# A two-stream encoder layer on one core: the gate input and the gate's mix rows kept in SBUF, the pivot subtracted behind the update, the first norm's mean taken off first

## The chip, the core and the metric

The kernel runs on one core of a Trainium2 chip. The metric is device time of one execution in microseconds. Three executions of the kernel before took 1427.2 (the median), 1424.3 and 1427.87 us. One more was taken with the hardware profiler.

## The reference: what is computed

One layer of a streaming encoder, for a prompt of 1024 frames and for 32 frames of a running stream, with the same weights, all in float32, model width 1024. The input is modulated, projected, handed to three groups of heads (an mLSTM with a matrix memory, FoX attention with forget gates, and a gated MLP), joined, projected back, and normalised; a SwiGLU block with a second norm follows.

```python
h = x * (1 + sc1) + sh1
mq, mk, mv, mo, mi, mf, fq, fk, fv, ff, gu, gv = jnp.split(h @ w_in, split_at, axis=-1)
...
vn = _layer_norm(gv, gmlp_ln_g, gmlp_ln_b)
hg = _spatial_gate(gu, vn, gmlp_ws, gmlp_bs)   # 128 frames at a time, 4 groups of 64 channels
mix = jnp.concatenate([hm.reshape(B, S, D_MLSTM).astype(dt),
                       hf.reshape(B, S, D_FOX).astype(dt), hg], axis=-1) @ w_o
x = _layer_norm(ALPHA * x + (1 + g1) * mix, ln1_g, ln1_b)
h = x * (1 + sc2) + sh2
y = (jax.nn.silu(h @ w_gate) * (h @ w_up)) @ w_down
x = _layer_norm(ALPHA * x + (1 + g2) * y, ln2_g, ln2_b)
```

The states of the heads and vn of the 32 running frames are outputs too.

## The kernel before, in words

**Operands.** Every large product is made of three: operand and weight are split into a high part (a cast, L106 for weights) and a low part (a subtract, L107), and PE adds high*high, high*low and low*high (L118 to L120 in gemm, L283 to L285 in tm_unit) into one PSUM bank. Banks are few: three of pool pg ("g"), two of pt ("t"), two for the heads' scores and one for their output.

**Frames.** The 1056 frames (1024 of the prompt and 32 running) are nine tiles of 128 for the projections into rows (tm units), and two groups of columns for all that follows: group 0 is the prompt's first half, 512 frames in two cuts of 256; group 1 is the rest, 544 frames in two cuts of 272.

**Stages.** First the modulation and the input projection. Then a list sets the order in which units are emitted: fm units give fox's q and k (q0 to q7), tm units give values and gates, f0 to f7 are fox heads and m0 to m3 mLSTM tiles, both for group 0, whose working tiles lie in a pool mx0:

```python
ORDER = "q0 f0 q1 a f1 a q2 f2 k0 k1p s a q3 f3 a v q4 f4 a q5 f5 o a m0 q6 f6 a m1 q7 m2 f7 a m3"
```

When the list is done, mx0 is closed, and the pools ph (operands of the output projection), pz (residual z) and p2 (small tiles "tmp", "sil" and others) are opened on the memory that is free then. Now z is loaded (wo_res), the operand tiles hh and hl are made, and mix rows k = 0 to 5 are loaded from the DRAM tensor dmix and split into hh and hl (wo_mix, L888 the cast and L889 the subtract). Four tm units follow: gv for tiles 0 to 3 (evac_gv), gmlp for tiles 0 to 3 (evac_gmlp), then both for tiles 4 to 8; two fm units for group 1; then mix rows 6 and 7 by wo_mix; then the output projection wo of group 0, one tile of 128 rows (m) and one cut after another, its first norm ln1, the mixers of group 1 with the first products of the SwiGLU block between (up), its second product (down), and in the middle of that block group 1's wo and ln1.

**Who sets the order.** The program is written in that order, but a scheduler at build time fixes the order of each engine by when it expects operands. So a unit emitted later can run between the rows of an earlier one, which mostly holds here: while fox and mLSTM wait for DVE and ACT, PE runs the tm units. An engine then runs its rows strictly in that order. A tile in a pool that takes over freed memory waits for the last reader of the tiles that it covers (reuse by tile).

**The gate.** evac_gv normalises one tile of gv: statistics and the product on DVE (L353, into a "traw" tile, of which there are two), gain (L354) and offset (L355) on POOL, then a store to the DRAM tensor dvn. evac_gmlp loads that tile again ("gvn"), copies u out of its bank (L645, "traw"), mixes 128 frames with four matmuls per tile (L650) and multiplies (L653). to_mix transposes the result (L632), copies it to "mixs" (L634) and stores it to dmix.

**The sublayer's end and the norms.** sublayer_end takes a wo or down bank: DVE's L927 adds bank times gate into z. To keep the sums of squares small, z carries a pivot: row tile m = 0 gives a mean over its 128 rows (L837 on PE, L838 on ACT), which is subtracted from z's tile 0 by DVE (L839) and from every other tile by POOL (L924), there ahead of L927. ln_sum gathers sums (L849) and squares (L851). ln_stats makes from them r, the reciprocal deviation (L863 to L869), and e = -mean * r (L870); ln1 then runs per k: z times r (L942, DVE), plus e (L943, six on DVE and two on POOL), scale and shift (L946, ACT), high part (L950, ACT), low part (L951, DVE), which are operands of up (up_g). ln1_res (L960) prepares z for the next residual.

## Time and profile before

| what | us |
|---|---|
| three executions, median | 1427.2 |
| the profiled execution's own time | 1432.34 |
| its span in the trace | 1430.6 |
| PE busy | 1366.2 |
| DVE busy | 1046.7 |
| ACT busy | 657.2 |
| POOL busy | 269.3 |
| f6's transposes to m3's in the trace | 310.7 to 364.6 |
| first matmul of group 0's wo | 389.1 |
| first wait of PE behind group 0's ln1 | 472.4 |
| group 0's last down group, PE's wait | 889 to 890.75 |

The span is that of one profiled execution on the core; the profiled execution's own time has 1.7 us more around it. Busy time is the time in which an engine has at least one instruction running; matmuls overlap in the pipeline, so a full PE has no gap between them. The rows of the trace name an engine, a line of the kernel, the tile written and the tiles read, without their serial numbers.

### The profile page before, as it was taken

How to read it: one execution, taken by the hardware profiler on the slowest of the kernel's cores; microseconds unless marked ns; L12 is line 12 of the kernel's file. 1: busy time of each engine (PE TensorE's matmuls, PEld its weight loads, DVE VectorE, ACT ScalarE, POOL GpSimd, SP SyncE). 2: the span in 40 equal slices, each digit the busy share in tenths (PEclk: the TensorE clock that was granted, in tenths of full speed). 3: DMA queues.
4: the chain of work that ended last, by engine and by line, in shares of the span. 5: the costliest groups of instructions: out<-in, count | busy, mean ns of one | idle time of the engine just before them, and what ended most of it. 6: DMA issues, size and time to landing. Idle time of an engine off the chain costs nothing.

```text
span 1430.6 us, 28812 instructions
## 1 busy us (share of the span) xinstructions
PE 1366.2 (96%) x10937; PEld 1312.7 (92%) x10937; DVE 1046.7 (73%) x2359; ACT 657.2 (46%) x1392; POOL 269.3 (19%) x313
## 2 busy tenths in 40 slices
PE   7999999999999899999999999999999999999994
PEld 4799988989889789999999998999898999999994
DVE  5548655678678677687777764678878877878777
ACT  3323234434445564546555453335655444536353
POOL 0103200043167300000000001174611000000343
PEclk9999999999999999999999998999999999999997
DMA  9754678465754745344343423565666666534231
GB/s 360 248 207 133 193 210 257 159 213 168 226 172 157 210 161 178 110 150 122 119 146 103 101 86 73 194 176 151 184 160 187 178 175 185 149 125 133 75 118 63
DMA packets 135986, 233.02 MB, mean 163 GB/s; under 512 B 22548, under 2 KB 79516, under 8 KB 135848
## 3 DMA queue, kind: packets, MB, share of 16 engines
q1 hardware_dynamic: 130952, 221.74, 48.9%
q0 software_dynamic: 4896, 9.44, 4.5%
q8 instruction: 86, 1.41, 0.4%
q14 instruction: 52, 0.43, 0.1%
HBM read 197.24 MB, written 52.76 MB: 175 GB/s over the span
## 4 chain that ended last, share of the span: by engine, by line
PE 75%; DVE 10%; DMA 8%; ACT 3%; issue 2%; SPq 1%; POOL 0%; DVEq 0%; ACTq 0%
PE up_g L119 5%; PE up_g L120 5%; PE up_g L118 5%; PE dn_g L118 4%; PE dn_g L119 3%; PE dn_g L120 3%; PE tm_g L283 3%; PE tm_g L284 3%; PE tm_g L285 3%; PE fm_g L118 3%; PE fm_g L119 2%; PE fm_g L120 2%; PE fox_t L733 2%; PE wo_g L120 2%; PE wo_g L118 2%
## 5 line engine op out<-in xcount | busy, mean ns | idle before, releaser
L119 PE MATMUL up_g<-wo_al,up_whi 128*128 128x256 f32 (+1 forms) x736 | 211.7, 288 | 3.8 <-DVE wo_al L951 3.8
L118 PE MATMUL up_g<-wo_ah,up_whi 128*128 128x256 f32 (+1 forms) x736 | 210.3, 287 | 3.9 <-ACT lna_tmp L946 3.3
L120 PE MATMUL up_g<-wo_ah,up_wlo 128*128 128x256 f32 (+1 forms) x736 | 210.4, 286 | 0.9 <-DVE up_wlo L107 0.9
L118 PEld LDWEIGHTS up_g<-wo_ah,up_whi 128*128 128x128 f32 x736 | 139.6, 190 | 5.4 <-ACT wo_ah L950 3.5
L119 PEld LDWEIGHTS up_g<-wo_al,up_whi 128*128 128x128 f32 x736 | 139.8, 190 | 5.0 <-DVE wo_al L951 4.2
L120 PEld LDWEIGHTS up_g<-wo_ah,up_wlo 128*128 128x128 f32 x736 | 139.7, 190 | 1.6 <-DVE up_wlo L107 1.4
L284 PE MATMUL tm_g<-tm_wlo,start_h1h 128*128 128x256 f32 (+1 forms) x384 | 110.6, 289 | 0.0
L285 PE MATMUL tm_g<-tm_whi,start_h1l 128*128 128x256 f32 (+1 forms) x384 | 110.3, 288 | 0.0
L283 PE MATMUL tm_g<-tm_whi,start_h1h 128*128 128x256 f32 (+1 forms) x384 | 109.8, 287 | 0.2 <-ACT tm_mixs L634 0.2
L118 PE MATMUL fm_g<-start_h1h,fm_whi 128*128 128x256 f32 (+2 forms) x344 | 102.2, 302 | 6.9 <-DVE fm_qkl L368 2.0
L118 PE MATMUL dn_g<-up_acth,dn_whi 128*128 128x256 f32 (+1 forms) x352 | 103.5, 295 | 2.7 <-DVE mlstm_z L927 2.4
L119 PE MATMUL dn_g<-up_actl,dn_whi 128*128 128x256 f32 (+1 forms) x352 | 101.6, 289 | 0.0
L120 PE MATMUL dn_g<-up_acth,dn_wlo 128*128 128x256 f32 (+1 forms) x352 | 101.6, 289 | 0.0
L119 PE MATMUL fm_g<-start_h1l,fm_whi 128*128 128x256 f32 (+2 forms) x344 | 101.6, 295 | 0.0
L120 PE MATMUL fm_g<-start_h1h,fm_wlo 128*128 128x256 f32 (+2 forms) x344 | 100.9, 295 | 0.0
L1057 ACT CAST sup_whi<-sup_raw 128x1024 fp32r<-128x1024 f32 x51 | 52.8, 1048 | 84.3 <-DVE sup_raw L1064 27.8
L107 DVE TENSOR_TENSOR up_wlo<-up_raw,up_whi 128x1024 fp32r<-128x1024 f32 x56 | 71.4, 1276 | 24.7 <-ACT up_whi L106 24.4
L106 ACT CAST up_whi<-up_raw 128x1024 fp32r<-128x1024 f32 x56 | 58.7, 1048 | 56.7 <-PE dn_g L119 20.6
L736 ACT CAST fox_pth<-fox_t 128x256 fp32r<-128x256 f32 (+3 forms) x144 | 51.0, 373 | 68.3 <-PE fox_t L733 63.4
L1058 DVE TENSOR_TENSOR sup_wlo<-sup_raw,sup_whi 128x1024 fp32r<-128x1024 f32 x51 | 63.9, 1256 | 18.5 <-ACT sup_whi L1057 18.4
L118 PEld LDWEIGHTS fm_g<-start_h1h,fm_whi 128*128 128x128 f32 x344 | 65.4, 192 | 12.4 <-ACT start_h1h L223 3.1
L737 DVE TENSOR_TENSOR fox_ptl<-fox_t,fox_pth 128x256 fp32r<-128x256 f32 (+3 forms) x144 | 58.0, 417 | 23.7 <-ACT fox_pth L736 22.5
(560 smaller groups left out, 4662.9 us busy)
## 6 DMA issues: line engine op xcount, KB each, us to landing
up_raw<-w_gu SPq DMA_DIRECT2D x56, 512.0 KB
dn_raw<-w_dn SPq DMA_DIRECT2D x28, 512.0 KB
ada_late<-w_ada SPq DMA_DIRECT2D x24, 512.0 KB
wo_raw<-w_o SPq DMA_DIRECT2D x24, 512.0 KB
start_dp<-w_gu SPq DMA_DIRECT2D x18, 512.0 KB
start_dp<-w_gu POOLq DMA_DIRECT2D x18, 512.0 KB, 7.1
sup_raw<-w_gu SPq DMA_DIRECT2D x17, 512.0 KB
sup_raw<-start_dp SPq DMA_DIRECT2D x17, 512.0 KB
```

The lines of the kernel that those rows point to most:

```text
L106: nc.scalar.copy(hi[:, :w], raw[:, :w])
L107: (eng or nc.vector).tensor_tensor(lo[:, :w], raw[:, :w], f(hi[:, :w]), ALU.subtract)
L118: nc.tensor.matmul(ps, hi, xh(k), start=start and k == 0, stop=False)
L119: nc.tensor.matmul(ps, hi, xl(k), start=False, stop=False)
L120: nc.tensor.matmul(ps, lo, xh(k), start=False, stop=stop and k == n - 1)
L283: nc.tensor.matmul(ps[:, :ncol], xh, hi, start=k == 0, stop=False)
L284: nc.tensor.matmul(ps[:, :ncol], xh, lo, start=False, stop=False)
L285: nc.tensor.matmul(ps[:, :ncol], xl, hi, start=False, stop=k == 7)
L736: nc.scalar.copy(ph[:, lo:nq], ps[:, lo:nq])
L737: nc.vector.tensor_tensor(pl[:, lo:nq], ps[:, lo:nq], f(ph[:, lo:nq]), ALU.subtract)
L1057: nc.scalar.copy(h, x)
L1058: tt(l, x, f(h), ALU.subtract)
```

## The change

The line numbers of the changed kernel are shifted: L355 becomes L360, L632 L636, L650 L660, L839 L849, L924 L961, L927 L958, L942 L975, L951 L983.

1. The offset of the gate norm is added into a tile that stays: for tiles 0 to 7 halves of "sil" tiles of p2 (two buffers, a tag that other units use later), for tile 8 a "gvn" tile. The nine stores to dvn and nine loads are gone; evac_gmlp reads the tile.
2. For tiles 0 to 3 of the gate to_mix writes the transposed rows straight into hh (ACT) and hl (DVE) at k = 6 and 7. Their four stores to dmix, four loads, and wo_mix(0, (6, 7)) with four casts and four subtracts are gone.
3. The pivot is subtracted on POOL behind L927 instead of ahead of it, in wo and in down's last group, for both groups of frames.
4. ln1 uses a new ln_center: ACT copies the mean to SBUF, and while r is being made, the mean is taken off z's eight tiles, on DVE and POOL in turn; behind r a single product per k is left. L870 and L943 are gone.

```diff
--- before.py
+++ after.py
@@ -352,10 +352,14 @@
         v = self.t(self.sm, [P, 256], F32, "traw", 2)
         nc.vector.tensor_scalar(v[:n], ps[:n, :256], mv[:n, 0:1], r[:n], ALU.subtract, ALU.mult)
         nc.gpsimd.tensor_tensor(v[:n], v[:n], self.rowp[:n, 272:528], ALU.mult)
-        nc.gpsimd.tensor_tensor(v[:n], v[:n], self.rowp[:n, 528:784], ALU.add)
-        self.store(self.dvn[:n, tt, :], v[:n])
         if tt == 8:
-            self.store(self.d["o_vn"], v[:n])
+            self.vn[tt] = self.t(self.sm, [P, 256], F32, "gvn", 1)
+        elif tt % 2 == 0:
+            x = self.t(self.p2, [P, 544], F32, "sil", 2)
+            self.vn[tt], self.vn[tt + 1] = x[:, :256], x[:, 256:512]
+        nc.gpsimd.tensor_tensor(self.vn[tt][:n], v[:n], self.rowp[:n, 528:784], ALU.add)
+        if tt == 8:
+            self.store(self.d["o_vn"], self.vn[tt][:n])
 
     def evac_qk(self, h):
         nc = self.nc
@@ -630,6 +634,13 @@
         ps = bank or self.t(self.pt, [P, 512], F32, "t")
         for i in range(2):
             nc.tensor.transpose(ps[:, i * P:i * P + L], x[:L, i * P:(i + 1) * P], self.ident[:L, :L])
+        if k0 == 6 and j < 4:
+            a = j // 2 * 256
+            y = ps[:, :256].rearrange("p (i q) -> p i q", i=2)
+            hi, lo = (z[0][a][:, 6:8, j * P - a:(j + 1) * P - a] for z in (self.hh, self.hl))
+            nc.scalar.copy(hi, y)
+            nc.vector.tensor_tensor(lo, y, f(hi), ALU.subtract)
+            return
         s = self.t(pool, [P, 2, P], F32, "mixs", 2)
         nc.scalar.copy(s[:, :, :L], ps[:, :256].rearrange("p (i q) -> p i q", i=2)[:, :, :L])
         c = min(j // 4, 1)
@@ -639,8 +650,7 @@
 
     def evac_gmlp(self, tt, ps, n, bank=None):
         nc = self.nc
-        vn = self.t(self.sm, [P, 256], F32, "gvn", 2)
-        self.load(vn[:n], self.dvn[:n, tt, :])
+        vn = self.vn[tt]
         u = self.t(self.sm, [P, 256], F32, "traw", 2)
         nc.scalar.copy(u[:n], ps[:n, :256])
         bank = bank or ps
@@ -850,6 +860,29 @@
                               z[:, m, sl], ALU.add)
         nc.vector.tensor_tensor(st["qs"][:, sl], st["qs"][:, sl], sq, ALU.add)
 
+    def ln_center(self, st, z, sl, sub):
+
+        nc = self.nc
+        n = sl.stop - sl.start
+        pm = self.t(self.pt, [P, 512], F32, "t")[:, :n]
+        nc.tensor.matmul(pm, self.onesm, st["zs"][:, sl], start=True, stop=True)
+        pq = self.t(self.pt, [P, 512], F32, "t")[:, :n]
+        nc.tensor.matmul(pq, self.onesm, st["qs"][:, sl], start=True, stop=True)
+        mean = st["zs"][:, sl]
+        nc.scalar.copy(mean, pm)
+        v = self.t(self.p2, [P, 272], F32, "tmp", 4)[:, :sl.stop - sl.start]
+        nc.scalar.activation(v, pm, AF.Square)
+        nc.vector.scalar_tensor_tensor(v, pq, self.epsa, v, ALU.add, ALU.subtract)
+        r = st["pv"][:, sl]
+        nc.scalar.activation(r, v, AF.Ln)
+        nc.scalar.activation(r, r, AF.Exp, scale=-0.5)
+        nc.vector.scalar_tensor_tensor(v, v, -0.5, r, ALU.mult, ALU.mult)
+        nc.vector.tensor_tensor(v, v, r, ALU.mult)
+        nc.vector.scalar_tensor_tensor(r, v, 1.5, r, ALU.add, ALU.mult)
+        for k in range(KT):
+            (nc.gpsimd if sub[k] == "p" else nc.vector).tensor_tensor(z[:, k, sl], z[:, k, sl], mean, ALU.subtract)
+        return r
+
     def ln_stats(self, st, sl):
 
         nc = self.nc
@@ -920,12 +953,12 @@
 
         sl = slice(a, b)
         pivot = st and st["pivot"]
-        if pivot and m:
-            self.nc.gpsimd.tensor_tensor(z[:, m, sl], z[:, m, sl], st["pv"][:, sl], ALU.subtract)
         g = self.modcol(gate, m)
         for x, y, i in self.parts(c, a, b):
             self.lastz = self.nc.vector.scalar_tensor_tensor(z[:, m, x:y], ps[:, x - a:y - a], g[i], z[:, m, x:y],
                                                              ALU.mult, ALU.add)
+        if pivot and m:
+            self.nc.gpsimd.tensor_tensor(z[:, m, sl], z[:, m, sl], st["pv"][:, sl], ALU.subtract)
         if pivot and m == 0:
             self.ln_pivot(st, z, sl)
         if st and st["sum"]:
@@ -934,13 +967,12 @@
     def ln1(self, c, st, a, b):
         self.phase = f"lna{c}"
         nc, z, hh, hl, sl = self.nc, self.z[c], self.hh[c][a], self.hl[c][a], slice(a, b)
-        r, e = self.ln_stats(st, sl)
+        r = self.ln_center(st, z, sl, "vpvpvpvp")
         for k in range(KT):
             yield
             self.phase = f"lna{c}"
             zk = z[:, k, sl]
             nc.vector.tensor_tensor(zk, zk, r, ALU.mult)
-            (nc.gpsimd if k % 4 == 1 else nc.vector).tensor_tensor(zk, zk, e, ALU.add)
             h = self.t(self.p2, [P, 272], F32, "tmp", 4)[:, :b - a]
             for x, y, i in self.parts(c, a, b):
                 nc.scalar.activation(h[:, x - a:y - a], z[:, k, x:y], AF.Identity, bias=self.lnb[:, k, i:i + 1],
@@ -1163,7 +1195,7 @@
         self.dmqk = t([P, 4, T], "dmqk")
         self.dmv = t([P, 9, 256], "dmv")
         self.dmo = t([P, 9, 256], "dmo")
-        self.dvn = t([P, 9, 256], "dvn")
+        self.vn = {}
         self.dfs = t([8, 6, S], "dfs")
         self.dsf = t([8, 2, PAST + NS], "dsf")
         self.dM = t([4, 9, P], "dM")
@@ -1277,7 +1309,6 @@
         for h in range(QD, PRE):
             self.fm_unit(w3[2 + h], self.evac_qk(h), (1,))
         s6.close()
-        self.wo_mix(0, self.KORDER[6:])
         self.pn = self.pool("pn")
         self.ln_consts()
         st = self.ln_begin(nc.gpsimd)
```

**PE, between fox's f6 and mLSTM's m3.** Rows of PE's order in the kernel before, behind the transposes of f6 and the first mLSTM products; fox_, mlstm_ and ada_ tiles belong to the list's units, tm_g is a bank of a tm unit, tm_gvn the reloaded gate input:

```order
L650 MATMUL tm_g_4638<-tm_gvn_4663,start_wsp_176 128x64 x4
L284 MATMUL tm_g_4680<-tm_wlo_4593,start_h1h_168 128x256
L285 MATMUL tm_g_4680<-tm_whi_4592,start_h1l_169 128x256
L283 MATMUL tm_g_4680<-tm_whi_4592,start_h1h_168 128x256
L284 MATMUL tm_g_4680<-tm_wlo_4593,start_h1h_168 128x256
L285 MATMUL tm_g_4680<-tm_whi_4592,start_h1l_169 128x256
L632 MATMUL tm_g_4596<-start_ident_120,tm_traw_4623 128x128 x2
L584 MATMUL mlstm_s_3942<-mlstm_mv_740_3905,mlstm_mkw_3929 128x130 x2
L186 MATMUL ada_t_3878<-start_ident_120,ada_adas_3891 128x128 x2
L553 MATMUL mlstm_s_4076<-mlstm_mqb_4055,mlstm_mqk_4053 128x256 x2
L632 MATMUL tm_g_4638<-start_ident_120,tm_traw_4665 128x128 x2
L283 MATMUL tm_g_4722<-tm_whi_4586,start_h1h_168 128x256
```

And in the changed kernel the end of that stretch, from f7's last products (fox_o) over m3's last rows (mlstm_t_4329) to the first tm row:

```order
L565 MATMUL mlstm_t_4282<-start_ident_119,mlstm_mqk_4255 128x128 x2
L748 MATMUL fox_o_4190<-fox_ptl_4223,fox_v_4136 64x128
L753 MATMUL fox_o_4190<-fox_pth_4222,fox_v_4136 128x128
L757 MATMUL fox_o_4190<-fox_pth_4196,fox_v_4136 128x512
L186 MATMUL ada_t_4234<-start_ident_119,ada_adas_4247 128x128 x2
L588 MATMUL mlstm_s_4298<-mlstm_mv_835_4261,mlstm_mkw_4285 128x130 x2
L636 MATMUL mlstm_t_4329<-start_ident_119,mlstm_mhm_4309 128x128 x2
L283 MATMUL tm_g_4632<-tm_whi_4583,start_h1h_167 128x256
L284 MATMUL tm_g_4632<-tm_wlo_4584,start_h1h_167 128x256
```

From f6's transposes to the L636 row there is no tm row left in the changed order: the tm banks from tm_g_4632 on, 296 matmuls of 128x256 with nine tiles of L660 and L636, stand behind it.

**POOL, over the same stretch.** In the kernel before, L354 (gain) and L355 (offset) of a gate tile stand together; mlstm_ rows are the list's units:

```order
L354 TENSOR_TENSOR tm_traw_4456<-tm_traw_4456,start_rowp_175 128x256
L355 TENSOR_TENSOR tm_traw_4456<-tm_traw_4456,start_rowp_175 128x256
L354 TENSOR_TENSOR tm_traw_4497<-tm_traw_4497,start_rowp_175 128x256
L355 TENSOR_TENSOR tm_traw_4497<-tm_traw_4497,start_rowp_175 128x256
L107 TENSOR_TENSOR tm_wlo_4593<-tm_raw_4590,tm_whi_4592 128x1024
```

In the changed kernel L360 is the offset, written to a "sil" tile (the gains L354 of the first two tiles, tm_traw_4455 and tm_traw_4496, stand further ahead):

```order
L546 TENSOR_TENSOR mlstm_mo_4061<-mlstm_mo_4061,start_rowp_174 128x256
L535 MEMSET mlstm_mv_835_4261 128x4
L546 TENSOR_TENSOR mlstm_mo_4264<-mlstm_mo_4264,start_rowp_174 128x256
L360 TENSOR_TENSOR tm_sil_4458<-tm_traw_4455,start_rowp_174 128x256
L360 TENSOR_TENSOR tm_sil_4458<-tm_traw_4496,start_rowp_174 128x256
L354 TENSOR_TENSOR tm_traw_4536<-tm_traw_4536,start_rowp_174 128x256
L354 TENSOR_TENSOR tm_traw_4577<-tm_traw_4577,start_rowp_174 128x256
```

The first two offsets moved behind the gates (mlstm_mo) of m2 and m3, and the third and fourth gate tile's rows behind them.

**DVE, at group 0's last down group.** In the kernel before, up_pv is the pivot and dn_g a bank of down:

```order
L107 TENSOR_TENSOR dn_wlo_12360<-dn_raw_12357,dn_whi_12359 128x1024
L839 TENSOR_TENSOR mlstm_z_856_4347<-mlstm_z_856_4347,up_pv_12152 128x256 x2
L927 SCALAR_TENSOR_TENSOR mlstm_z_856_4347<-dn_g_12195,start_mod_155,mlstm_z_856_4347 128x256
L927 SCALAR_TENSOR_TENSOR mlstm_z_856_4347<-dn_g_12231,start_mod_155,mlstm_z_856_4347 128x256
L927 SCALAR_TENSOR_TENSOR mlstm_z_856_4347<-dn_g_12261,start_mod_155,mlstm_z_856_4347 128x256
```

In the changed kernel:

```order
L107 TENSOR_TENSOR dn_wlo_12317<-dn_raw_12314,dn_whi_12316 128x1024
L958 SCALAR_TENSOR_TENSOR mlstm_z_855_4346<-dn_g_12188,start_mod_154,mlstm_z_855_4346 128x256
L958 SCALAR_TENSOR_TENSOR mlstm_z_855_4346<-dn_g_12203,start_mod_154,mlstm_z_855_4346 128x256
L849 TENSOR_TENSOR mlstm_z_855_4346<-mlstm_z_855_4346,up_pv_12109 128x256
L958 SCALAR_TENSOR_TENSOR mlstm_z_855_4346<-dn_g_12218,start_mod_154,mlstm_z_855_4346 128x256
L958 SCALAR_TENSOR_TENSOR mlstm_z_855_4346<-dn_g_12233,start_mod_154,mlstm_z_855_4346 128x256
```

Two updates moved ahead of the first cut's subtract L849, and the second cut's subtract moved further back.

## The prediction

> **What bounds the kernel now.** I read the page first, then the table of stretches around the stages that the change touches, then the waits of the tensor engine, and last single pieces of the timeline. The page:
>
> ```profile
> span 1430.6 us, 28812 instructions
> PE 1366.2 (96%) x10937; PEld 1312.7 (92%) x10937; DVE 1046.7 (73%) x2359; ACT 657.2 (46%) x1392; POOL 269.3 (19%) x313
> PE   7999999999999899999999999999999999999994
> PEclk9999999999999999999999998999999999999997
> ```
>
> PE is busy 96% of the span, in nearly every slice. So the kernel is bound by PE's own stream, and a change can pay only through the 64 us in which PE stands idle, or through the clock. It can cost without such a limit, wherever it leaves PE without work. PE's waits on what the change touches:
>
> ```profile
> engine line waited for: us in total, times, longest us
> PE up_g L119 <- DVE wo_al L951: 3.8, 2, 3.2
> PE up_g L118 <- ACT lna_tmp L946: 3.3, 1, 3.3
> PE dn_g L118 <- DVE mlstm_z L927: 2.4, 2, 1.8
> PE tm_g L650 <- DMA tm_gvn<-start_dvn: 1.9, 1, 1.9
> PE wo_g L118 <- DVE mlstm_z L927: 1.3, 1, 1.3
> PE wo_g L118 <- ACT wo_whi L106: 1.0, 1, 1.0
> PE wo_g L120 <- DVE wo_wlo L107: 0.8, 1, 0.8
> ```
>
> **Part 1, the gate input in SBUF: a loss.** This is the term that decides. By the order of instructions, the gate unit's matmuls (tm_g: input projection L283 to L285, token mix L650, transposes L632) are spread in before between the last fox and mLSTM units (f6, m1, m2, f7, m3). In the changed kernel all of them but the first three gate tiles stand behind m3's last transposes. The reason lies in the code: the add of the gate norm now writes a "sil" tile of pool p2, which is opened on the memory of the fox/mLSTM pool mx0 after that is closed. The first such add (POOL) must wait until the tiles under it are read for the last time. Behind it on POOL stand the next tiles' L354 and adds; the two "traw" buffers stay full, so DVE's L353 of the next tiles waits, their PSUM banks stay taken, and PE has no bank to fill.
>
> What that stretch holds in before, from f6's transposes (310.7 us) to m3's (364.6). The first row is of the stretches (its length, then busy time of PE, PEld, DVE, ACT and POOL with their counts, granted clock, DMA share, GB/s), the next five are PE's groups on tm_g (count, then least, median and greatest ns, first and last start), the last two of the timeline:
>
> ```profile
> 310.70:364.60 53.90, 53.76 (x448) 50.12 (x447) 45.97 (x159) 23.61 (x64) 16.45 (x19) 1.00 0.50 152
> L285 PE MATMUL tm_g<-tm_whi,start_h1l x79: 276/282/367, 310.5 to 362.9; 128*128 128x256 f32 x79
> L283 PE MATMUL tm_g<-tm_whi,start_h1h x78: 274/282/367, 310.6 to 359.1; 128*128 128x256 f32 x78
> L284 PE MATMUL tm_g<-tm_wlo,start_h1h x78: 276/282/369, 310.8 to 359.2; 128*128 128x256 f32 x78
> L650 PE MATMUL tm_g<-tm_gvn,start_wsp x48: 217/275/323, 317.4 to 363.8; 128*128 128x64 f32 x48
> L289 PE MATMUL tm_g<-tm_whi,start_hs x8: 276/278/467, 345.2 to 347.2; 128*64 128x256 f32 x8
> 366.18 0.28 PE L283 MATMUL tm_g<-tm_whi,start_h1h 128*128 128x256 f32 x1
> 366.30 0.28 PE L284 MATMUL tm_g<-tm_wlo,start_h1h 128*128 128x256 f32 x1
> ```
>
> PE is full there (53.76 of 53.90 us). Matmuls of this shape start 0.12 us apart. The filler is 78 + 78 + 79 + 16 (the rows of the short tile, L288 to L291, together) = 251 x 0.119 = 29.9 us; the 48 of L650 and eight transposes (L632) at about 0.11 = 6.0. Together 35.9. What remains, 53.8 - 35.9 = **17.9 us, is the fox and mLSTM units' own PE work**.
>
> How long does the stretch take without filler? It is a chain through DVE, ACT and PE, and DVE carries most. DVE's rows there:
>
> ```profile
> L653 DVE SCALAR_TENSOR_TENSOR tm_traw<-tm_g,start_colp,tm_traw 128x64 f32<-128x64 f32 x23 | 5.1, 277 | 1.4 <-PE tm_g L650 1.3
> L737 DVE TENSOR_TENSOR fox_ptl<-fox_t,fox_pth 128x512 fp32r<-128x512 f32 (+3 forms) x8 | 3.8, 480 | 1.3 <-ACT fox_pth L736 1.3
> L548 DVE SCALAR_TENSOR_TENSOR mlstm_mw<-mlstm_mb,start_col,start_maskbig 128x128 f32<-128x128 f32 x8 | 3.1, 444 | 1.9 <-PE mlstm_s L569 1.9
> L591 DVE SCALAR_TENSOR_TENSOR fm_C<-fm_C,fm_d0c,mlstm_s 64x65 f32<-64x65 f32 x8 | 2.2, 280 | 0.1
> L188 DVE TENSOR_REDUCE ada_adam<-ada_t 128x4 f32<-128x16 f32 x1 | 0.2, 173 | 0.0
> L539 ACT ACTIVATE mlstm_mo<-mlstm_mo 128x256 f32<-128x256 f32 x2 | 0.8, 417 | 2.5 <-DMA mlstm_mo<-start_dmo 2.5
> ```
>
> The groups of tm_ and fm_wlo tiles (first row: L653) sum to 19.2 us. The other 28 groups (second row to the L188 row) sum to 34.6, and a third L591 block of 1.1 that now also comes ahead of the filler makes 35.7. Neighbours overlap a little in the records (54 us of rows in 46 us of busy time), so the **floor** is 46.0 - 19.2 = 27. The **ceiling** is the 53.9 us that the stretch takes with filler. On the chain the instructions follow each other, so I take their sum and add the waits that are not the filler's: 1.3 us (L737 on ACT), about 1.4 of small ones, and 2.5 for the reload of the output gate (L539). That is 40.9. I take **40 us**, in which PE has 17.9 us of work: **22 us idle** (bounds 9 and 36). The 36 us of filler aren't hidden any more; they are run afterwards, so this idle time arrives in full at the output projection.
>
> Two smaller losses. First, the restart: in ACT's new order five casts of wo_mix (L921) stand ahead of L641, which empties the third gate tile's bank. They wait for loads that SP issues behind eight loads of z. One such load of each kind in before:
>
> ```profile
> 368.70 4.91 DMA mlstm_z<-xT
> 392.63 5.18 DMA wo_tmp<-start_dmix
> ```
>
> So a wait of one load is about 5 us, and part of it runs while PE still has two free banks. I take 3 us (0 to 6). Second, the clock:
>
> ```profile
> 890.75 0.51 PE L118 MATMUL dn_g<-up_acth,dn_whi 128*128 128x256 f32 x1 [1.75 <-DVE mlstm_z L927]
> 891.06 0.42 PE L119 MATMUL dn_g<-up_actl,dn_whi 128*128 128x256 f32 x1
> 891.28 0.41 PE L120 MATMUL dn_g<-up_acth,dn_wlo 128*128 128x256 f32 x1
> 890.00:900.00 10.00, 8.60 (x57) 8.40 (x58) 4.20 (x8) 1.73 (x4) 9.16 (x14) 0.83 0.67 171
> 470.00:480.00 10.00, 6.10 (x40) 5.60 (x39) 9.42 (x21) 8.05 (x19) 7.61 (x9) 0.89 0.35 115
> ```
>
> Behind a pause the matmuls start 0.21 us apart, and the granted clock of the ten-microsecond row is 0.83: a window at half speed that costs 1.7 us. The row at 470 us shows 1.1 us lost so, before its window runs on into the next row. A stretch in which PE works 18 of 40 us should see several such windows; only their matmuls on the chain count, plus one window when the filler starts again. I take 3 us (0 to 9, half of the 17.9 again).
>
> The Trainium skill, "TensorE: Matmul & The Clock Gate", sections "What's actually happening" and "HAM oscillation", says that the array falls to half rate after an idle window of about 3.4 us and regains full rate after as long of sustained work. This speaks against the change. The trace agrees on the size of one such window (10 us at 0.83, 1.7 us lost); by the page no window would be lost if every pause stays below 3.4 us, and the clock term would be 1.7 us or nothing instead of 3.
>
> In return the wait for the reload of the gate (tm_gvn) goes: -1.9. The 9 stores and 9 loads themselves lie beside PE work and cost SP only.
>
> **Part 2, mix rows 6 and 7 straight into the operand.** The three wo_g waits above (1.0, 0.8, 1.3 us) come of the last mix loads: in the chain of work the load quoted last (392.63 us, 5.18 us) is followed by the weight splits and the first update that PE then waits for. The load holds up ACT's and DVE's queues by its four casts and subtracts, and the weight splits (L106, L107) stand behind. It goes: **-3.1**. ACT copies and DVE subtracts take the place of the ACT copy to "mixs" and of L888 and L889, so no engine gains work.
>
> **Part 3, pivot off behind the update.** In down's last group (g=4) DVE's z0 subtract (L839) and POOL's pivot subtracts stood ahead of the first updates, and PE's banks were full. In the new order L958 updates stand ahead of both. The wait of 2.4 us goes, and the half-speed window behind it (1.7): **-4** (bounds -4.1 and 0, if the subtracts come back later on).
>
> ```profile
> L924 POOL TENSOR_TENSOR mlstm_z<-mlstm_z,wo_pv 128x256 f32<-128x256 f32 x14 | 14.7, 1086 | 12.4 <-ACT wo_pv L838 12.4
> ```
>
> In the wo stages PE is the bound, and I cost the edit at 0: a tile's 24 matmuls, 2.9 us at 0.12, cover one update on DVE and one such subtract of 1.1 us on POOL; at the stage's end, where no further tile covers it, it could add that 1.1 us ahead of the sums.
>
> **Part 4, mean off first.**
>
> ```profile
> 469.10 2.44 DVE mlstm_z L942 x6
> ...
> 471.70 1.00 DVE mlstm_z L942 x2
> ...
> 472.93 0.42 DVE mlstm_z L943
> 473.38 0.61 ACT lna_tmp L946
> ```
>
> For group 0's second cut ACT's first output waits for eight products (L942) and then an add (L943). Now the mean subtracts stand ahead of r, the row L870 goes, and the first ACT row needs one product alone: it starts some 4 us sooner. ACT then paces it at about 1 us for each k. PE's 3.3 us wait and half-speed window shrink: **-4** (0 to -5). For group 1 the wait on wo_al (3.2 us) had L951 behind a DVE row waiting for a load; now the L983 rows stand ahead, but the wait for up_wlo on a like load remains and may grow by as much: **-1.5** (-3.2 to +3).
>
> **Sum**, against the profiled execution's own 1432.3 us: +22 + 3 + 3 - 1.9 - 3.1 - 4 - 4 - 1.5 = +13.5, so 1445.8. That execution stands 5.1 us above the median of the runs shown, 1427.2; so 1445.8 - 5.1 = **1441 us**.
>
> **The rivals.**
> - *The stretch is cheap* (other side, faster). One mechanism: DVE, rid of 19 us of filler, runs the stretch at near its floor. At 27 us PE idles 9; with no restart or clock loss and the gains at their values, 9 - 14.5 = -5.5: 1422. It decides below 17.9 + 14.5 = 32 us without, or 26 us with, the restart and clock terms. For it: DVE was 85% busy there. Against it: single-tile dependences and the 2.5 us reload don't shrink.
> - *The throttle and the queues make it worse.* The stretch takes 46 us because PE's links of the chain run at half speed, and the restart stalls 6: 28 + 6 + 3 - 14.5 = +22.5: 1450; at its ceiling 1458.
> - *The change doesn't do what it says*: gate tiles go to SBUF but the add runs early after all, since only the order, not a wait, holds it. PE's order is fixed at build and stands as read, so only small shifts are possible; then loss and gain come out even, about 1427.
>
> **How the numbers follow.** Forecast 0.55, worse 0.22, cheap stretch 0.13, even 0.10. About 0.3% (4.3 us) is what a measurement can tell from no change. The forecast's own range is 1432 to 1449. The range of 8 in 10 reaches from 1424 to 1457: it leaves out the lower half of the cheap case and the end of the worse one. Faster 0.13, same 0.10, slower 0.77.
>
> **What would show it.** Right: between f6's and m3's transposes PE stands well below half busy for some 40 us with a granted clock under 1, and the gate's matmuls come in one block behind it; no tm_gvn or mix load in the wo stage's waits; no wait at down's last group; the LN wait of 3.3 us gone or near 1. Wrong: PE filled there, or a stretch below 32 us; or the waits of LN and down merely moved a few rows on.

## The result, and the profile after

The changed kernel takes **1457.6 us** (median of five, 1454.9 to 1462.5) against 1427.0 of the kernel before in the same comparison: ratio 1.0224, 95% interval 1.0203 to 1.0244. It is slower, as forecast, but by 31 us where 14 were forecast. The page of its profiled execution:

```profile
span 1460.7 us, 28736 instructions
PE 1382.9 (95%) x10937; PEld 1324.5 (91%) x10937; DVE 1044.4 (71%) x2347; ACT 658.0 (45%) x1392; POOL 280.2 (19%) x321
PE   7999999977899899999999999999999999999994
PEclk9999999996999999999999999999999999999997
```

Slices 9 to 11 stand out: PE is at 7, 7 and 8 tenths, with a granted clock of 6 in the middle one. The same stretch in steps of 10 us (columns as in the prediction):

```profile
310.00:320.00 10.00, 6.37 (x53) 4.59 (x51) 8.49 (x31) 3.66 (x9) 0.13 (x1) 1.00 0.53 169
320.00:330.00 10.00, 7.24 (x26) 6.07 (x26) 4.75 (x15) 2.59 (x7) 1.35 (x3) 0.57 0.37 103
330.00:340.00 10.00, 6.84 (x19) 4.40 (x19) 9.02 (x34) 3.28 (x11) 0.00 (x1) 0.50 0.11 28
340.00:350.00 10.00, 7.41 (x39) 4.96 (x38) 6.92 (x20) 3.80 (x11) 2.28 (x3) 0.50 0.09 27
350.00:360.00 10.00, 7.08 (x40) 6.47 (x37) 4.37 (x18) 1.70 (x4) 2.79 (x4) 0.72 0.33 95
360.00:370.00 10.00, 5.84 (x47) 5.14 (x45) 3.60 (x14) 2.71 (x9) 0.00 (x0) 0.96 0.74 248
```

PE runs 19 to 53 instructions in 10 us where before ran 78 to 89, and busy time deceives: at half clock each instruction lasts longer. Of PE's waits, those that bear on the change; the first row is of the kernel before:

```profile
PE fm_g L118 <- DVE fm_qkl L368: 2.0, 1, 2.0
```

```profile
PE fm_g L118 <- DVE fm_qkl L372: 6.1, 2, 3.7
PE mlstm_s L557 <- DMA mlstm_mqk<-start_dmqk: 5.0, 1, 5.0
PE tm_g L636 <- DVE tm_traw L663: 4.0, 3, 2.2
PE tm_g L283 <- DVE tm_traw L353: 2.9, 1, 2.9
PE dn_g L118 <- DVE mlstm_z L958: 0.7, 1, 0.7
PE up_g L119 <- DVE wo_al L983: 0.2, 1, 0.2
```

The waits of tm_gvn and the mix loads are gone, down's fell from 2.4 to 0.7, group 0's norm's (3.3) and wo_al's (3.8) are gone or 0.2. New are the waits for a load of m2 (mlstm_mqk), ahead of the gate tiles' transposes (L636) and ahead of the first matmul into a gate bank (L283); the wait of fm_g for fm_qkl grew from 2.0 to 6.1. So the waits that the change aimed at went, and others came. By stage, with wo's, up's and the second norm's first matmuls as marks:

| stage, us | before | after | difference | forecast |
|---|---|---|---|---|
| start to first wo matmul of group 0 | 389.1 | 424.5 | +35.4 | +26 |
| wo of group 0 | 50.0 | 46.8 | -3.2 | -3 |
| end of that wo to first up matmul | 27.6 | 33.4 | +5.8 | |
| first up matmul to wo of group 1 | 453.7 | 446.1 | -7.6 | -8 with the row above |
| wo of group 1 | 48.6 | 48.6 | 0 | 0 |
| from there to the second norm | 91.6 | 93.1 | +1.5 | -1.5 |
| rest | 370.0 | 368.2 | -1.8 | 0 |

The differences add up to the spans': 1460.7 - 1430.6 = 30.1. Each column is one profiled execution, and small differences say little: in kernels with the same code up to there, wo began at 385.3 to 392.8 us; first up matmul to wo of group 1 took 448.7 to 453.7 in those without parts 3 and 4 in group 0; and the changed kernel, profiled again, had 91.5 in the last row but one. Only the end of wo to the first up matmul is steady: 27.0 to 28.2 in all runs without parts 3 and 4 there, 33.2 to 33.5 in all with both.

### The profile page after: what moved, and what is told of

Read it like the earlier page. It is cut to its first block, busy times and chain, and to the rows that moved or that the text cites. A ratio compares the mean times of both kernels' runs of the same rounds, so it can differ in the third digit from the quotient of the medians.

```text
span 1460.7 us, 28736 instructions
## 1 busy us (share of the span) xinstructions
PE 1382.9 (95%) x10937; PEld 1324.5 (91%) x10937; DVE 1044.4 (71%) x2347; ACT 658.0 (45%) x1392; POOL 280.2 (19%) x321
## 4 chain that ended last, share of the span: by engine, by line
PE 48%; DVE 9%; DMA 5%; ACT 4%; issue 3%; POOL 3%; SPq 0%; DVEq 0%; ACTq 0%; POOLq 0%
PE up_g L118 5%; PE up_g L119 5%; PE up_g L120 5%; PE dn_g L118 3%; PE dn_g L119 3%; PE dn_g L120 3%; PE sup_u L118 2%; PE sup_u L120 2%; PE sup_u L119 2%; PE fox_t L743 2%; PE sup_g L118 1%; PE sup_g L120 1%; PE sup_g L119 1%; POOL mlstm_z L961 1%; PE dn_u L118 1%
## 5 line engine op out<-in xcount | busy, mean ns | idle before, releaser
L283 PE MATMUL tm_g<-tm_whi,start_h1h 128*128 128x256 f32 (+1 forms) x384 | 111.5, 292 | 2.9 <-DVE tm_traw L353 2.9
L107 DVE TENSOR_TENSOR up_wlo<-up_raw,up_whi 128x1024 fp32r<-128x1024 f32 x56 | 71.9, 1283 | 29.7 <-ACT up_whi L106 29.1
L283 PEld LDWEIGHTS tm_g<-tm_whi,start_h1h 128*128 128x128 f32 x384 | 74.6, 195 | 5.3 <-DVE tm_traw L353 3.2
```

What stands on the lines that cost most here:

```text
L107: (eng or nc.vector).tensor_tensor(lo[:, :w], raw[:, :w], f(hi[:, :w]), ALU.subtract)
L283: nc.tensor.matmul(ps[:, :ncol], xh, hi, start=k == 0, stop=False)
```

## Experiments: what holds the filler back

**Part 1 alone, part 2 alone** (the kernel before, with that part's lines of the diff and no others).

> Before with part 1 alone (the gate input in sil tiles). Theory A: the reuse of the fox/mLSTM memory alone holds the filler back, so PE is under 80% busy between f6's and m3's transposes, wo starts near 424 us as in the changed kernel, and the last mix loads' 3 us wait may return: 1455 to 1463 us. Theory B: parts 1 and 2 each hold back a share of the filler: 1437 to 1447 us. Theory C: the loss sits in the norms and the pivot, and this run is 1422 to 1430 us.

> Before with part 2 alone (mix rows 6 and 7 written straight into the operand). Theory A as I gave it in the prediction (only the sil memory blocks): the filler stays hidden and the 3.1 us of mix waits go, about 1424 us. Theory A2: the operand tiles lie on the fox/mLSTM memory too, so the banks of three gate tiles stay taken until m3 ends, and all but some 50 matmuls (6 us) of the filler come late: 1445 to 1456 us.

Measured: part 1 alone 1459.1 us, ratio 1.0213 (1.0182 to 1.0243); part 2 alone 1451.4, ratio 1.0159 (1.0129 to 1.0189). Each alone costs most of the loss. From f6's to m3's transposes in these two kernels, part 1's first:

```profile
309.20:351.20 42.00, 30.03 (x144) 21.66 (x142) 29.95 (x102) 14.28 (x39) 3.78 (x7) 0.63 0.27 78
```

```profile
309.50:356.00 46.50, 38.13 (x223) 30.20 (x221) 34.65 (x119) 15.23 (x42) 4.56 (x9) 0.71 0.32 97
```

PE has 144 and 223 instructions there instead of 448. Theory A holds for part 1, A2 for part 2: the operand hh and hl lies on the memory of the fox/mLSTM pool too, so three gate banks stay taken. In the run with part 2 alone PE had transposed three gate tiles at 322.2, 323.9 and 331.2 us; ACT emptied their banks only behind m3's last copy (L641):

```profile
356.03 0.37 ACT L641 COPY mlstm_mixs<-mlstm_t 128x256 f32<-128x256 f32 x1 [0.52 <-PE mlstm_t L632]
356.30 0.93 ACT L637 CAST mlstm_ah<-tm_g 128x256 fp32r<-128x256 f32 x3
```

The prediction named only the first of these two locks (waits for memory).

**The gate in memory of its own.** The small pool sm exists since the start; four tiles fit.

```diff
-        if tt == 8:
-            self.vn[tt] = self.t(self.sm, [P, 256], F32, "gvn", 1)
-        elif tt % 2 == 0:
-            x = self.t(self.p2, [P, 544], F32, "sil", 2)
-            self.vn[tt], self.vn[tt + 1] = x[:, :256], x[:, 256:512]
+        if tt == 8:
+            self.vn[tt] = self.t(self.p2, [P, 544], F32, "sil", 2)[:, :256]
+        else:
+            self.vn[tt] = self.t(self.sm, [P, 256], F32, "gvn", 4)
```

> Part 1 alone, but with the gate input in four tiles of the small pool that exists since the start (the 32-frame tile in p2). Theory A (the loss is the wait for the fox/mLSTM memory): the order has its filler back, PE is full between f6 and m3, 1423 to 1430 us. Rival (keeping the gate input in SBUF costs by itself, through POOL's order or the lost DRAM buffer): 1440 us or more.

> The changed kernel with the gate input in tiles of their own. Theory A2 (the operand tiles of part 2 lie on the same memory and block by themselves): some 50 matmuls of filler come back, the rest stays behind m3: 1448 to 1455 us. Rival (the sil tiles alone block): 1430 us or less.

Measured: 1427.0 us, ratio 1.0006 (0.9991 to 1.002), for part 1 alone; 1456.5, ratio 1.0209 (1.0184 to 1.0234), for the whole change with these tiles, a little above its range. The first one's stretch:

```profile
310.00:365.00 55.00, 54.94 (x459) 51.36 (x459) 47.44 (x162) 24.28 (x67) 16.42 (x20) 1.00 0.37 108
```

PE is full again, at full clock. Keeping the gate input in SBUF costs nothing that this can tell; the memory that it was put on did. It gains nothing either: the 1.9 us wait for tm_gvn doesn't show in the total. With part 2 added, its lock alone brings the loss back.

## Experiments: the clock and the tail

**Is it the half clock?** The trace shows one run of 30.7 us at half clock in the stretch. In "warm" PE gets work of no use (its result is read by nothing); warm2 adds 16 more such matmuls each ahead of the transposes in to_mix, for gate tiles 0 to 3.

```diff
         st = self.t(self.pss, [P, 512], F32, "s")
+        if 0 < j < 4:
+            for _ in range(24):
+                nc.tensor.matmul(st[:, :256], self.h1parts(0, P)[0](0), self.h1parts(0, 256)[0](0), start=True, stop=True)
...
         nd = self.t(self.pss, [P, 512], F32, "s")
+        if 0 < j < 4:
+            for _ in range(8):
+                nc.tensor.matmul(nd[:, :256], self.h1parts(0, P)[0](0), self.h1parts(0, 256)[0](0), start=True, stop=True)
```

> The changed kernel with 24 matmuls of no use ahead of the first products of m1, m2 and m3 and 8 ahead of the second (96 matmuls of 128x256, 11.5 us of PE work at full clock; nothing reads them). Theory K (the half clock is what I sized too small): with PE kept busy the clock stays at 1.0 over most of the stretch, stretch and restart shrink by 5 to 10 us, the whole is 1447 to 1453 us. Rival (the chain is DVE's and the loads', the clock costs nothing): 1457 us or more, as the added work stands in PE's order.

> As the run with added matmuls in m1 to m3, and 16 more of them ahead of the transposes of each of gate tiles 0 to 3 (64 in all, 7.7 us at full clock; nothing reads them), where PE stood waiting for DVE in the tail. Theory T (the tail's half-speed windows, some 10 us long, cost 5 us, and come of the waits for the gate tiles): the windows between 355 and 385 us go, and although 7.7 us are added, the whole is 1455 to 1460 us, no slower than with the first set alone. Rival (the clock in the tail costs nothing, the work is added in full): 1464 us or more.

Measured: warm 1459.4 us, ratio 1.0223 (1.0189 to 1.0258); warm2 1468.3, ratio 1.029 (1.026 to 1.0319). The stretch and the tail (m3's transposes to wo) of the changed kernel, and of warm:

```profile
310.25:352.80 42.55, 30.40 (x145) 22.03 (x143) 30.05 (x102) 14.28 (x39) 3.77 (x7) 0.64 0.25 75
352.80:424.50 71.70, 63.05 (x483) 61.01 (x483) 36.02 (x107) 21.96 (x53) 15.08 (x19) 0.93 0.40 126
```

```profile
309.60:352.50 42.90, 32.48 (x230) 26.77 (x228) 31.96 (x114) 14.51 (x39) 4.24 (x8) 0.90 0.27 78
352.50:423.50 71.00, 63.90 (x484) 61.48 (x483) 31.62 (x95) 22.36 (x53) 15.07 (x19) 0.89 0.40 124
```

The clock rose from 0.64 to 0.90, and the stretch stayed at 42.6 and 42.9 us. **Theory K is not borne out**: the whole is no faster. But the run doesn't show that the half clock costs nothing. PE's busy time in the stretch stays about the same, 30.4 and 32.5 us: the added matmuls, 11.5 us at full clock by the estimate above, take up what the half clock had stretched. And the end of the stretch hangs on another engine in each. First the changed kernel, m3's last products (L588) and transposes (L636) on PE and the row of DVE (L626) that makes the operand of the transposes; then the same three in warm (L594, L642, L632):

```profile
351.95 0.69 PE L588 MATMUL mlstm_s<-mlstm_mv,mlstm_mkw 128*128 128x130 f32 x4
352.48 0.38 PE L636 MATMUL mlstm_t<-start_ident,mlstm_mhm 128*128 128x128 f32 x2
349.73 0.43 DVE L626 TENSOR_TENSOR mlstm_mhm<-mlstm_mhm,mlstm_mo 128x256 f32<-128x256 f32 x1
```

```profile
346.67 0.71 PE L594 MATMUL mlstm_s<-mlstm_mv,mlstm_mkw 128*128 128x130 f32 x4
352.15 0.66 PE L642 MATMUL mlstm_t<-start_ident,mlstm_mhm 128*128 128x128 f32 x2 [4.77 <-DVE mlstm_mhm L632]
351.57 0.43 DVE L632 TENSOR_TENSOR mlstm_mhm<-mlstm_mhm,mlstm_mo 128x256 f32<-128x256 f32 x1
```

In the changed kernel the operand is there at 350.2 us and waits 2.3 us for PE's own rows, at half clock; in warm PE is through some 5 us sooner and then waits for DVE, whose rows stand in another order. So what the half clock costs in the stretch stays open. warm2 came out slower than warm, so theory T is not borne out; that run adds work to the waits it meant to fill, so it does not clear the clock in the tail either.

**Is it the queues?** In the tail ACT and PE of the changed kernel stand like this:

```profile
366.01 1.36 ACT L921 CAST mlstm_ah<-wo_tmp 128x256 fp32r<-128x256 f32 x4 [5.24 <-DMA wo_tmp<-start_dmix]
369.33 0.37 ACT L641 CAST mlstm_ah<-tm_g 128x256 fp32r<-128x256 f32 x1
```

```profile
367.12 0.44 PE L636 MATMUL tm_g<-start_ident,tm_traw 128*128 128x128 f32 x2 [2.18 <-DVE tm_traw L663]
368.89 0.47 PE L636 MATMUL tm_g<-start_ident,tm_traw 128*128 128x128 f32 x2 [1.33 <-DVE tm_traw L663]
```

ACT waits 5.2 us for a mix load, and the cast that frees a gate bank (L641) stands behind. z_late only emits z's loads later (`wo_res` behind the q and k units):

> The changed kernel with the loads of z emitted behind the gate units, so that SP issues the first four mix loads ahead of z. Theory Q (the restart's waits are ACT's and DVE's queues behind mix loads that stand behind 2 MB of z): the first mix casts run some 3 to 5 us sooner, 1452 to 1455 us. Rival (the loads wait for dmix and for memory, not for z): 1457 to 1459 us.

Measured: 1459.4 us, ratio 1.0235 (1.0207 to 1.0264): no gain. The mix casts did come sooner, the first at 355.9 us, but in that order all twelve stood ahead of L641. So in z_after the mix loads are also held behind the gate:

```diff
-        self.wo_res(0, self.pz)
         self.operand(0, self.ph)
-        self.wo_mix(0, self.KORDER[:6])
...
+        with tc.issue_after(self.lastgm.ins):
+            self.wo_mix(0, self.KORDER[:6])
+            self.wo_res(0, self.pz)
         for h in range(QD, PRE):
```

Here lastgm is to_mix's subtract of gate tile 3. Four mix casts are left ahead of L641.

> The changed kernel with z loaded behind the first four mix loads, and only four mix casts ahead of the casts that empty the gate tiles' banks (eight follow them). Theory Q2 (in the tail the banks wait in ACT's queue behind mix casts, some 6 us of idle and the half-speed windows that follow): wo starts 6 to 9 us sooner than in the changed kernel, 1448 to 1452 us. Rival (the tail's idle has other causes): 1456 us or more.

> The changed kernel again, on one chip with the next run, so that the two can be set side by side: 1455 to 1460 us.

> The run with four mix casts ahead of the gate banks' casts and z behind them, again. Theory Q2 (the tail's excess comes of ACT's queue): 4 to 7 us below the changed kernel on this chip. Rival (its profile's 5.7 us earlier start of wo was chance): within 2 us of it.

Measured: z_after 1455.5 us, ratio 1.0187 (1.0159 to 1.0216); then side by side on one chip the changed kernel 1461.3 (1.0213 to 1.0265) and z_after again 1456.9 (1.0185 to 1.0234). The medians lie 4.4 us apart, as theory Q2 asks, though the intervals overlap. The two profiled executions lie 8.1 us apart, so the rows show more than the medians do. Their tails, the changed kernel's first:

```profile
352.80:426.40 73.60, 66.65 (x500) 64.30 (x497) 36.94 (x110) 23.01 (x55) 15.10 (x19) 0.90 0.39 122
```

```profile
352.80:418.10 65.30, 60.25 (x483) 58.41 (x484) 34.30 (x102) 21.70 (x52) 17.53 (x19) 0.97 0.44 137
```

PE's idle time in the tail falls from 6.9 to 5.1 us and the clock rises from 0.90 to 0.97. PE's wait ahead of the gate tiles' transposes (L636) is 0.4 us in z_after2, 2.2 and 4.0 in the two profiles of the changed kernel. So part of the tail is ACT's queue, with the pauses and, as far as the clock goes with them, the half-speed windows behind it. How much of that is clock and how much waiting is not settled.

## Experiments: pivot and norm

**Part 3 alone, part 4 alone** (the kernel before with that part of the diff).

> Before with part 3 alone (pivot behind the update). As predicted: down's last group no longer waits 2.4 us and loses no half-speed window, 1423 us. Rival: what is gained there comes back as another wait, 1426 to 1428 us.

> Before with part 4 alone (mean off first). As predicted: group 0's norm 4 us sooner and group 1's 1.5, 1421 to 1422 us. Rival from the changed kernel's trace: the mean subtracts crowd DVE while PE's banks wait for q and k to be emptied, so the gain behind the norm is given back ahead of it, 1426 to 1430 us.

Measured: part 3 alone 1429.4 us, ratio 1.0008 (0.9989 to 1.0028); part 4 alone 1428.9, ratio 1.0001 (0.9983 to 1.0019). Both rivals hold, part 3's a little above its range. Where part 3's gain goes stands in POOL's and DVE's rows at the end of wo in that run (L948 is the update):

```profile
442.40 0.47 DVE L948 SCALAR_TENSOR_TENSOR mlstm_z<-wo_g,start_mod,mlstm_z 128x256 f32<-128x256 f32 x1
445.10 0.61 DVE L851 TENSOR_TENSOR wo_qs<-wo_qs,wo_tmp 128x256 f32<-128x256 f32 x1 [1.08 <-ACT wo_tmp L848]
445.63 0.47 DVE L948 SCALAR_TENSOR_TENSOR mlstm_z<-wo_g,start_mod,mlstm_z 128x256 f32<-128x256 f32 x1
446.04 1.22 DVE L107 TENSOR_TENSOR fm_wlo<-fm_raw,fm_whi 128x1024 fp32r<-128x1024 f32 x1
448.34 0.62 DVE L851 TENSOR_TENSOR wo_qs<-wo_qs,wo_tmp 128x256 f32<-128x256 f32 x1 [1.08 <-ACT wo_tmp L848]
```

```profile
446.18 1.68 POOL L951 TENSOR_TENSOR mlstm_z<-mlstm_z,wo_pv 128x256 f32<-128x256 f32 x1 [0.76 <-DVE mlstm_z L948]
447.94 0.74 POOL L849 TENSOR_TENSOR wo_zs<-wo_zs,mlstm_z 128x256 f32<-128x256 f32 x1
```

And the last two updates in the kernel before:

```profile
437.63 0.47 DVE L927 SCALAR_TENSOR_TENSOR mlstm_z<-wo_g,start_mod,mlstm_z 128x256 f32<-128x256 f32 x1
440.03 0.47 DVE L927 SCALAR_TENSOR_TENSOR mlstm_z<-wo_g,start_mod,mlstm_z 128x256 f32<-128x256 f32 x1
```

Update, subtract of 1.7 us and sum now follow each other, and the norm starts behind them. The subtract also holds up the next tile: in DVE's order the sum of squares (L851) stands ahead of the next update and waits 1.08 us for it. So the updates come 3.2 us apart where 2.4 was the last distance before, slower than PE's 2.9 us for a tile, and the last one starts 2.7 us behind wo's last matmul (442.97) where it was 0.7 (439.32). The end of wo to up took 30.8 us in that run (27.6 before), up to wo of group 1 446.7 (453.7). If that is so, the pivot moved in down alone must pay:

```diff
-        if pivot and m:
+        if pivot and m and gate == "g1":
             self.nc.gpsimd.tensor_tensor(z[:, m, sl], z[:, m, sl], st["pv"][:, sl], ALU.subtract)
         g = self.modcol(gate, m)
...
+        if pivot and m and gate == "g2":
+            self.nc.gpsimd.tensor_tensor(z[:, m, sl], z[:, m, sl], st["pv"][:, sl], ALU.subtract)
```

> Before with the pivot behind the update in down's last group alone; wo as before. Theory P (part 3 pays some 4 us in down and gives 3 back at the end of wo, where subtract and sum follow the last update on POOL): 1422 to 1424 us. Rival (the gain in down doesn't reach the end): 1426 to 1428 us.

Measured: 1422.7 us, ratio **0.9959** (0.9940 to 0.9978). It pays 5 to 6 us. Theory P holds: in its profile the wait at down's last group is gone, and the end of wo to up took 27.9 us, as before.

**The norm.** First the row that ends r in the kernel before; then DVE in the changed kernel, behind wo's last matmul at 471.5 us:

```profile
445.38 0.87 DVE L869 SCALAR_TENSOR_TENSOR wo_pv<-lna_tmp,wo_pv 128x256 f32<-128x256 f32 x1
```

```profile
475.68 3.58 DVE L883 TENSOR_TENSOR mlstm_z<-mlstm_z,fm_zs 128x256 f32<-128x256 f32 x4
480.05 0.47 DVE L875 SCALAR_TENSOR_TENSOR lna_tmp<-lna_t,start_epsa,lna_tmp 128x256 f32<-128x256 f32 x1
482.99 0.85 DVE L881 SCALAR_TENSOR_TENSOR fm_pv<-lna_tmp,fm_pv 128x256 f32<-128x256 f32 x1
483.76 2.18 DVE L883 TENSOR_TENSOR mlstm_z<-mlstm_z,fm_zs 128x256 f32<-128x256 f32 x3
485.86 2.96 DVE L975 TENSOR_TENSOR mlstm_z<-mlstm_z,fm_pv 128x256 f32<-128x256 f32 x8
489.08 1.41 DVE L107 TENSOR_TENSOR fm_wlo<-fm_raw,fm_whi 128x1024 fp32r<-128x1024 f32 x1
490.41 0.49 DVE L372 SCALAR_TENSOR_TENSOR fm_qkl<-fm_g,start_qsc,fm_qkh 128x272 fp32r<-128x272 f32 x1
```

r (L881) is there 12.3 us behind wo's end. In before it is there (L869) at 446.25, 6.8 us behind wo's last matmul at 439.4. DVE's half of the mean subtracts, 3.6 us, stands ahead of L875, with which the making of r begins. Then the second cut's mean subtracts stand ahead of the first cut's products, and the row that empties PE's bank of q and k (L372) behind them all: PE waits 3.7 us for it. A half-speed window follows (clock 0.83 from 490 to 500 us), so the wait of up and its window moved here. Two more runs, part 4 alone with `"pppppppp"` in place of `"vpvpvpvp"`, and with ln_center for group 1 only:

> Before with part 4 alone, all eight mean subtracts on POOL. Theory D (part 4 gives back its gain because the subtracts on DVE keep DVE from emptying PE's banks of q and k): without them on DVE the 3.6 us wait for fm_qkl shrinks and the predicted gain shows, 1421 to 1424 us. Rival (eight of them on POOL, 0.74 us each and more, end later than r and delay the products): 1427 us or more.

> Before with the mean taken off first in group 1's norm alone. Theory N (part 4 pays in group 1, where it stood 3 us shorter in the run with part 4 alone, and gives its gain back in group 0): 1423 to 1425 us. Rival (group 1's stage is held by up_wlo behind the loads either way): 1426 to 1428 us.

Measured: 1433.5 us, ratio 1.0053 (1.0032 to 1.0074); and 1427.5, ratio 0.999 (0.9974 to 1.0005). Theory D falls: with no subtract on DVE it is slower, and the wait for fm_qkl stays at 3.5 us. In that run r is there at 450.2 us, 7.5 behind wo's last matmul, so DVE's subtracts were what had held it; but the eight products behind it, beside POOL's subtracts, take 6.98 us where the changed kernel's took 2.96:

```profile
450.32 6.98 DVE L965 TENSOR_TENSOR mlstm_z<-mlstm_z,wo_pv 128x256 f32<-128x256 f32 x8
453.45 7.83 POOL L873 TENSOR_TENSOR mlstm_z<-mlstm_z,wo_zs 128x256 f32<-128x256 f32 x8
```

Theory N isn't shown: group 1's norm alone pays nothing that this can tell.

**Putting together.** own_pl is parts 1 (own tiles), 3 and 4; own_early is the own tiles, with the loads of rows 6 and 7 emitted behind gate tiles 0 to 3 (`if i == 2: self.wo_mix(0, self.KORDER[6:])` in the loop over the gate units); best is own_early with the pivot moved in down alone and the mean first in group 1 alone.

> Parts 1, 3 and 4 with the gate input in tiles of their own, mix rows 6 and 7 through DRAM as before. If parts 3 and 4 each pay what I predicted (4 and 5.5 us) and the filler is back: 1418 to 1420 us. If, as each alone showed, their gains are given back: 1425 to 1429 us.

> Gate input in tiles of their own; mix rows 6 and 7 still through DRAM, but their loads are emitted behind gate tiles 0 to 3 instead of behind the whole gate and two q and k units. Theory M (the 3.1 us of waits at the first wo tile come of the late mix loads, not of the DRAM path): they go without the direct write, 1422 to 1424 us. Rival (the waits come of weight splits and queues as well): 1425 to 1428 us.

> Gate input in tiles of their own, mix loads 6 and 7 emitted early, pivot behind the update in down alone, mean first in group 1 alone. If theories P and N hold and add: 1418 to 1421 us. If neither pays: 1425 to 1427 us.

Measured: own_pl 1429.2 us, ratio 1.0016 (1.0000 to 1.0032); own_early 1425.6, ratio 0.9989 (0.9970 to 1.0007); best **1421.8**, ratio 0.9944 (0.9927 to 0.9961). So parts 3 and 4 give their gains back beside the filler too (own tiles without them: 1.0006), and theory M is not borne out. Best beats both kernels, a little above the range for both theories together; its interval overlaps that of the pivot in down alone, so what the other parts add is not shown.

## Why the prediction was wrong in size

- **Part 1, the mechanism: right.** PE ran 145 instructions between f6 and m3 instead of 448, the gate came in one block behind, and own tiles brought all of it back. That it was the memory and not the order by itself is shown by the runs with own tiles. One sign did not come as stated: PE was not below half busy, as half clock stretched its work to 30.4 of 42.6 us.
- **Part 2 costed as a pure gain of 3.1: wrong.** The step "no engine gains work" looked at engines and not at where the operand lies: alone the part costs 1.0159. The 3.2 us did vanish from wo, but part 1 alone, which keeps the mix loads, has a wo of 46.4 us too: the delayed wo no longer meets them. The direct write did not earn it.
- **The stretch, 40 us: nearly right.** m3's transposes came after 42.2 us. PE waited 5.0 us for m2's load, where the prediction had counted 2.5 for another load; that this makes the difference is likely and not shown. The first filler matmul came 3.3 us later still, behind L353.
- **The clock term, 3 us, and the restart, 3 us: too small together.** The tail took 71.7 us where the terms make 24.5 + 35.9 - 1.9 + 3 = 61.5, some 64 with the clock term. The runs with reordered casts took 4.4 us of that back. In the stretch the clock was at half for 30.7 us; what that cost is open.
- **Parts 3 and 4, -9.5 together: failed, as their costs were put at nothing.** Each alone measured no gain (1.0008 and 1.0001), and so did both together with own tiles (1.0016). The step that failed for part 3 is that a tile's 24 matmuls, 2.9 us, cover one update and one subtract: the updates came 3.2 us apart, and at the end nothing covers a subtract of 1.68 us. For part 4 the subtracts on DVE stand ahead of r and of the rows that empty the banks of q and k. Together that is +5.8 between wo and up. The waits in down and behind the norm did go, but that the next stage is 7.6 us shorter, near the forecast of 8, is in part chance: kernels without these parts differ by 5 us there.
- **Sum.** Against the forecast by stage: +9.3 ahead of wo, +6.2 in the next two stages, +3 in group 1 (which a second profile doesn't repeat), -1.8 in the rest: 16.7 us, which carried the time just past the range's upper end of 1457. By parts: part 1 alone costs 30.7 us (1459.1 against 1428.45 in that comparison) where its terms make 22 + 3 + 3 - 1.9 = 26.1, and parts 2 to 4, forecast at -12.6, add nothing to that. So the gains that did not come weigh more than the tail. The rival with the throttle and the queues had 1458 as its ceiling, which the range left out; the time came near it by other terms than that rival's stretch of 46 us.

## What to carry to other kernels

Before moving a buffer from DRAM into SBUF, ask whose memory it takes and when that is last read: a tile on memory that is still in use is a wait, and a few buffers behind it can keep a whole filler stream from running. Price a moved operation where nothing follows to cover it, at the end of a stage, and not only where it was in the way. A gain in one stage is believed when the next stage's start moves too; testing the edit in one of its places alone showed the gain that the whole edit hid.

## What the runs showed of the hardware

The clock stayed at half for 30.7 us on end (321.4 to 352.1) while PE worked and paused by turns; 96 added matmuls lifted it to 0.90 on the mean of the stretch. The Trainium skill, "TensorE: Matmul & The Clock Gate", section "What's actually happening", speaks of an idle window of about 3.4 us for the fall and of a busy one for the return. The trace agrees for this fall, in a pause of 5.0 us, but not for all: the next one, at 355.5 us, lies in a pause of 2.9 us, and the one quoted in the prediction follows a pause of 1.75 us. In the kernel before the clock even fell at 880.6 us with no pause of PE from 872 to 888, behind 3 us of small matmuls (128x32 and 32x130). So a pause below 3.4 us is no safeguard here, and how many such windows fall into a stage differs from kernel to kernel where their code is the same: from the first up matmul to wo of group 1 the granted clock shows four in the kernel before, two with part 2 alone and five with part 1 alone in own tiles, each worth 1.7 us.

On DVE a 128x256 subtract with two SBUF inputs took 0.82 us on the mean of eight beside POOL's subtracts. Products of the same shape took 0.49 on the mean of nine with POOL idle or at other work part of the time:

```profile
L883 DVE TENSOR_TENSOR mlstm_z<-mlstm_z,fm_zs 128x256 f32<-128x256 f32 x8 | 6.2, 819 | 0.0
L975 DVE TENSOR_TENSOR mlstm_z<-mlstm_z,fm_pv 128x256 f32<-128x256 f32 x9 | 3.8, 486 | 0.0
```

The same product in the run with all subtracts on POOL came every 0.87 us (6.98 for eight, above). POOL's subtracts took 0.92 on the mean there, against 0.73 at the least (L961), and the pivot's 1.68 stands beside a row of DVE of 1.22 (L107). The Trainium skill, "SBUF — State Buffer", section "Who interferes with whom", says that a DVE instruction with two SBUF inputs contends with a GpSimd (POOL) instruction that reads SBUF, as its second input comes through a read interface that the two share; the durations agree with that.
